# Down projection of a gated FFN: 512 output columns a PSUM bank in place of 256, and unit by unit over four banks in the second block of a pair

## The chip, the cores and the metric

The kernel runs on one core of a Trainium2 chip. The metric is the device time of one execution in microseconds. Three executions of the kernel before took 2626.48, 2628.86 and 2635.57 us (median 2628.86). The profile is of one further execution, which took 2622.47 us; the span between its first and last instruction is 2620.6 us.

The engines are named as in the profile: PE (TensorE, matmuls; PEld is its weight loads), DVE (VectorE), ACT (ScalarE), POOL (GpSimd) and SP (the queue that issues most loads).

## The reference

One decoder step over a prompt of 2048 rows (plus 16 meta rows) and 8 sample rows, model width 1024. After the mixer comes a gated convolutional FFN of width 2816, and its last product is the place of this change:

```python
def conv_ffn(x, w_up, conv_w, conv_b, w_down, buf):
    l = x.shape[1]
    hid = x @ w_up
    a, v = hid[..., :D_FF], hid[..., D_FF:]
    ext = jnp.concatenate([buf.astype(a.dtype), a], axis=1)
    c = conv_b + sum(ext[:, j:j + l] * conv_w[j] for j in range(CONV_W))
    y = (jax.nn.silu(c) * v) @ w_down
    return y, ext[:, -(CONV_W - 1):]

def block(h, ...):
    ...
    yf, conv = conv_ffn(rms_norm(h, norm_ffn_g), ffn_w_up, ffn_conv_w, ffn_conv_b, ffn_w_down, conv0)
    return h + yf, s5r, s5i, hg, conv
```

A final RMSNorm of `h + yf` gives `y_prompt` (2048 x 1024) and `y_sample` (8 x 1024). All of it is float32.

## The kernel before

The prompt is cut into four blocks of 512 rows. The FFN is computed for two blocks at a time (`ffn(p2)`, first pair: blocks 0 and 1, second pair: blocks 2 and 3). In the code that pair is `blks`, and `ex` is true in the first pair, which also carries the 8 sample rows.

Every float32 operand is split into a rounded part and its rest: `split_w` (L446) makes `wh` on ACT (L449) and `wl` on DVE (L83) from a staged weight tile `st`; activations are `ah` and `al`, the gated product is `gh` and `gl`. A product is then three matmuls (`PASS`, L470): wh with gh, wh with gl, wl with gh. A weight tile that is loaded, split and used is called a unit (`w_unit`, L456): at most 128 x 1024 elements. There are two buffers of `st`, three of `wh` and three of `wl`.

The 2816 FFN columns are 22 tiles of 128, taken in six parts (`FPARTS`, L32: four of four tiles, two of three). For each part the up projection (`up`, `fm_mm`, matmuls at L480, up to 512 columns each, one PSUM bank of the pool `mm` at a time) gives `gh` and `gl` of the part for both blocks. Then the down projection adds the part's share to `hacc` (L1197 to L1218). Before the change it runs over four quarters of 256 output columns. A unit holds the part's tiles times 256 columns. For each block, two row tiles of 128 share a bank of 512: `tm_mm` (matmuls at L500) fills its left half with 12 matmuls (9 in parts of three tiles), then its right half, and DVE adds the bank to `hacc` (L80). In the very last part of the second pair the quarters are grouped as (0), (1, 2, 3), so that `finish` (the final norm and the output) of the first row tiles can begin early. In the first pair the sample rows follow each quarter as 40 stationary columns (`ex_mm`, L514; 40 = 8 high parts, padding, 8 low parts).

Where the first pair ends, the norms of blocks 2 and 3 (`norm2`, transposes at L547 into the pool `tp`) are asked for before the last down projection, and their instructions stand between its matmuls.

PSUM has eight banks: three of `mm` (`bank`), two of `tp` (`tbank`), three of `hg` (`gbank`); the FFN of the kernel before uses none of `hg`. The order of the instructions on each engine is made by a scheduler from the program and its dependencies, not by the order of the code alone.

Of the kernel before, what the change touches and what calls it, by code (L numbers as in the profile page):

```python
# [27 lines left out]
NF = 22  # L28
# [9 lines left out]
def kernel(  # L38
# [28 lines left out]
    def ap(t, off, pat):  # L67
        return bass.AP(tensor=t.tensor, offset=t.offset + off, ap=pat)
# [7 lines left out]
    mm = nc.tensor.matmul  # L76
    f_ = lambda a: a.bitcast(F32)

    def add(o, a, b):
        tt_(o, a, b, op=OP.add)  # L80
# [7 lines left out]
    def bank():  # L88
        return ps.tile([128, 512], F32, name="mm")
# [17 lines left out]
    def scr(shape=None):  # L107
        return shaped(nt.tile([128, 512], F32, name="nt"), shape)

    def v3(t, a, b):  # L110
        return t[:, :a * b].rearrange("p (a b) -> p a b", a=a)
# [334 lines left out]
    def split_w(st, n):  # L446
        hi = wp.tile([128, 1024], F32R, name="wh", bufs=3)
        lo = wp.tile([128, 1024], F32R, name="wl", bufs=3)
        ACT(hi[:, :n], st[:, :n], AF.Copy)  # L449
        sub(lo[:, :n], st[:, :n], f_(hi[:, :n]))  # L450
        return hi, lo

    def w_stage():
        return wp.tile([128, 1024], F32, name="st", bufs=2)

    def w_unit(src, k0, nk, c0, ncol):  # L456
        st = w_stage()
        rs = src.shape[1]
        dma_w(v3(st, nk, ncol), ap(src, k0 * 128 * rs + c0, [[rs, 128], [128 * rs, nk], [1, ncol]]))
        hi, lo = split_w(st, nk * ncol)  # L460
        return v3(hi, nk, ncol), v3(lo, nk, ncol)

    win, wglu, wout, wup, wdn = w_in[0], s5_w_glu[0], w_out[0], ffn_w_up[0], ffn_w_down[0]
# [6 lines left out]
    PASS = ((0, 0), (0, 1), (1, 0))  # L470
# [15 lines left out]
    def behind(ins, prev):  # L486

        if prev is not None:
            tc.add_manual_dep(ins.ins, prev.ins.name, mybir.DependencyInfo(
                mybir.DependencyClass.NoSync, mybir.DependencyReason.DATA), reason="bank shared by groups")  # L490
        return ins

    def tm_mm(dst, wu, nks, lhs, prev):

        i, tot = 0, 3 * sum(nks)
        k = 0
        for (hi, lo), nk in zip(wu, nks):
            for kk in range(nk):
                for wi, ai in PASS:
                    o = mm(dst, lhs(ai, k), (hi, lo)[wi][:, kk, :], start=(i == 0), stop=(i == tot - 1))  # L500
                    if i == 0:
                        behind(o, prev)
                    i += 1
                k += 1
        return o

    def ex_mm(dst, wu, nks, stat, m):

        i, tot = 0, 2 * sum(nks)
        k = 0  # L510
        for (hi, lo), nk in zip(wu, nks):
            for kk in range(nk):
                for w in (hi, lo):
                    mm(dst[:m], stat[:, k, :m], w[:, kk, :], start=(i == 0), stop=(i == tot - 1))  # L514
                    i += 1
                k += 1
# [9 lines left out]
    def norm_rows(x, m, sq=None):  # L526
        ss = sm.tile([128, 1], F32, name="ss", bufs=6)
        if sq is None:
            sq = scr().bitcast(mybir.dt.bfloat16)[:, :D]
        ACT(sq[:m], x[:m] if len(sq.shape) == 2 else v3(x, 8, 128)[:m], AF.Square, accum_out=ss[:m])  # L530
        return rstd_of(ss[:m], 1, 1.0 / D)
# [49 lines left out]
    def ex_sum(p, m, off, n):  # L581

        t = scr()[:m, :n]
        ACT(t, p[off:off + m, :n], AF.Copy)
        return t
# [504 lines left out]
    def ffn(p2):  # L1090
        blks = (2 * p2, 2 * p2 + 1)
        ex = p2 == 0
        acts, hacc = [F2[b] for b in blks], []
        if ex:
            hE = ex2.tile([10, D], F32, name="hE")
# [14 lines left out]
        def finish(b, ha, t):  # L1110
            r = norm_rows(ha[:, t], 128)
            stt(ha[:, t], ha[:, t], r, fng, op0=OP.mult, op1=OP.mult)
            (dma if ex else dma_w)(y_prompt[0, b * BT + t * 128:b * BT + t * 128 + 128, :], ha[:, t])

        def conv_tail():
            po = tbank()
            nc.tensor.transpose(po[:44, :128], aC.rearrange("p f j -> p (f j)"), ident)
            so = scr()[:44, :128]
            nc.vector.tensor_copy(so, po[:44, :128])
            dma(cv_p[0, 0].rearrange("j (f p) -> f j p", p=128), so)  # L1120

        for f0, f1 in FPARTS:
            nf = f1 - f0
            gs = {}
# [43 lines left out]
            if f0 == 0:  # L1168
                for b in blks:
                    ha = hp.tile([128, 4, D], F32, name="hacc")  # L1170
# [5 lines left out]
            if ex:  # L1176
# [11 lines left out]
                gst = ex2.tile([128, 4, 40], F32R, name="gst")  # L1188
# [3 lines left out]
            if f1 == NF:  # L1192
                fng = x4()
                dma_w(fng, ap(final_norm_g, 0, [[0, 128], [1, D]]))
                if not ex:
                    conv_tail()
            for qg in ((0,), (1, 2, 3)) if f1 == NF and not ex else ((0,), (1,), (2,), (3,)):  # L1197
                wus = [(slice(256 * q, 256 * q + 256), [w_unit(wdn, f0, nf, 256 * q, 256)]) for q in qg]
                for b, ha in zip(blks, hacc):
                    for t2_ in range(2):  # L1200
                        for qs, wu in wus:
                            p = v3(bank(), 2, 256)
                            o = None
                            for i in range(2):
                                t = 2 * t2_ + i
                                o = tm_mm(p[:, i, :], wu, (nf,),
                                          lambda ai, k: gs[b, f0 + k][ai][:, t * 128:t * 128 + 128], o)
                            hs = ha[:, 2 * t2_:2 * t2_ + 2, qs]
                            add(hs, hs, p)
                        if qg[-1] == 3 and f1 == NF:  # L1210
                            finish(b, ha, 2 * t2_)
                            finish(b, ha, 2 * t2_ + 1)
                for qs, wu in wus if ex else ():
                    pe = bank()
                    ex_mm(pe[:, :256], wu, (nf,), gst, 40)
                    t = ex_sum(pe, 8, 32, 256)
                    add(t, pe[:8, :256], t)
                    add(hE[0:8, qs], hE[0:8, qs], t)  # L1218
        if ex:
            r = norm_rows(hE, 8)  # L1220
            stt(hE[0:8], hE[0:8], r, fng[0:8], op0=OP.mult, op1=OP.mult)
# [11 lines left out]
    for p2 in range(2):  # L1233
        ffn(p2)
# [34 lines left out]
```

## Time and profile before

| | |
|---|---|
| median of three executions | 2628.86 us (2626.48 to 2635.57) |
| the profiled execution | 2622.47 us, span 2620.6 us, 39925 instructions |
| PE busy | 2496.9 us, 95% of the span |
| PEld, DVE, ACT, POOL busy | 86%, 56%, 34%, 6% |
| chain that ended last, by engine | PE 72%, DVE 11%, ACT 4%, DMA 3%, issue 3% |
| chain, by line | L480 (up projection and other products) 41%, L500 (down projection and others) 25% |
| TensorE's clock over the span | 0.987 of full speed |

How to read it: the busy time of PE is that of a pipeline. A matmul starts before the one ahead of it has ended, so the durations of single matmuls overlap, and the pace of the engine is the distance from one start to the next. The chain lists runs of matmuls with the time they took together, from which that distance follows. The two lines of the chain are helpers; L500 serves the FFN's down projection and, earlier, the mixer's products, and the names of the operands tell them apart (gh and gl are the FFN's).

### The profile page before, as it was taken

The page shows a single profiled execution, that of the slowest core. Times are in us where ns is not written, and L with a number is a line of the kernel's source. Part 1 is how long each engine was busy: PE and PEld are TensorE (multiplying, and loading weights), DVE is VectorE, ACT ScalarE, POOL GpSimd, SP SyncE. Part 2 cuts the span into 40 slices and gives each one's busy share as a digit, 9 for nine tenths or more (in the row PEclk, how much of TensorE's full clock was granted, in tenths as well). Part 3 has the DMA queues.
Part 4 walks back from the last instruction along what each step waited for, and adds up shares of the span by engine and source line. Part 5 has one row for each costly group of instructions (what it writes and reads, how often), then busy time and mean ns, then how long its engine had stood idle before and what let it go on. Part 6 is the DMA issues. An engine that isn't in the chain of part 4 may idle for free.

```text
span 2620.6 us, 39925 instructions
## 1 busy us (share of the span) xinstructions
PE 2496.9 (95%) x16515; PEld 2263.8 (86%) x16515; DVE 1456.0 (56%) x2978; ACT 903.6 (34%) x1564; POOL 166.2 (6%) x254
## 2 busy tenths in 40 slices
PE   7887998999999999999999999999999999999998
PEld 6786876888888888989999999999889898989887
DVE  6875697678669688553333333345843333343344
ACT  3553344434425445341313131223531313131222
POOL 1232100100000001000000000000300000000000
PEclk9997999999999999999999999999999999999999
DMA  4345433553564662731111111111521111111111
GB/s 126 103 138 184 98 111 133 153 167 121 132 197 131 168 219 86 247 92 49 49 45 45 49 48 42 43 47 57 195 73 49 49 49 49 49 49 49 41 48 74
DMA packets 274939, 252.50 MB, mean 96 GB/s; under 512 B 11367, under 2 KB 255999, under 8 KB 270654
## 3 DMA queue, kind: packets, MB, share of 16 engines
q1 hardware_dynamic: 264680, 220.42, 27.9%
q0 software_dynamic: 9904, 29.48, 3.5%
q8 instruction: 129, 2.11, 0.3%
q14 instruction: 52, 0.43, 0.1%
q10 hardware_dynamic: 174, 0.06, 0.0%
HBM read 216.41 MB, written 33.27 MB: 95 GB/s over the span
## 4 chain that ended last, share of the span: by engine, by line
PE 72%; DVE 11%; ACT 4%; DMA 3%; issue 3%; POOL 1%; SPq 0%; POOLq 0%; ACTq 0%; DVEq 0%
PE mm L480 41%; PE mm L500 25%; DVE wl L83 1%; DVE hf L632 1%; PE mm L514 1%; DMA st<-in_w_out_dram 1%; POOL rstd L521 1%; DVE sB L86 1%; DMA st<-in_w_in_dram 1%; PE tp L899 1%; ACT wh L449 1%; DVE sA L885 1%; DVE al L83 1%; PE tp L847 1%; DVE sA L86 1%
## 5 line engine op out<-in xcount | busy, mean ns | idle before, releaser
L480 PE MATMUL mm<-ah,wh 128*128 128x512 f32 (+3 forms) x2320 | 817.6, 353 | 5.1 <-ACT ah L552 3.8
L480 PE MATMUL mm<-al,wh 128*128 128x512 f32 (+3 forms) x2320 | 814.6, 351 | 1.1 <-DVE al L83 1.1
L480 PE MATMUL mm<-ah,wl 128*128 128x512 f32 (+3 forms) x2320 | 814.9, 351 | 0.5 <-DVE wl L83 0.5
L449 ACT ACTIVATE wh<-st 128x1024 fp32r<-128x1024 f32 (+1 forms) x264 | 275.7, 1046 | 859.8 <-PE mm L480 315.5
L480 PEld LDWEIGHTS mm<-ah,wh 128*128 128x128 f32 x2320 | 441.1, 190 | 60.0 <-ACT ah L552 4.5
L480 PEld LDWEIGHTS mm<-ah,wl 128*128 128x128 f32 x2320 | 441.1, 190 | 55.7 <-DVE wl L83 1.0
L480 PEld LDWEIGHTS mm<-al,wh 128*128 128x128 f32 x2320 | 441.0, 190 | 54.6 <-DVE al L83 1.6
L83 DVE TENSOR_TENSOR wl<-st,wh 128x1024 fp32r<-128x1024 f32 (+1 forms) x264 | 318.1, 1206 | 272.6 <-ACT wh L449 271.4
L500 PE MATMUL mm<-wh,gh 128*128 128x256 f32 x1408 | 399.6, 284 | 2.0 <-DVE hacc L80 1.5
L500 PE MATMUL mm<-wh,gl 128*128 128x256 f32 x1408 | 399.5, 284 | 0.0
L500 PE MATMUL mm<-wl,gh 128*128 128x256 f32 x1408 | 399.2, 284 | 0.0
L500 PE MATMUL mm<-wh,ah 128*128 128x256 f32 x1024 | 291.7, 286 | 7.3 <-ACT hg L671 3.2
L500 PE MATMUL mm<-wh,al 128*128 128x256 f32 x1024 | 290.9, 284 | 5.8 <-DVE al L83 5.0
L500 PE MATMUL mm<-wl,ah 128*128 128x256 f32 x1024 | 289.0, 284 | 1.2 <-DVE wl L83 1.2
L80 DVE TENSOR_TENSOR hacc<-hacc,mm 128x512 f32<-128x512 f32 x192 | 131.3, 685 | 267.1 <-PE mm L500 267.0
L500 PEld LDWEIGHTS mm<-wh,gh 128*128 128x128 f32 x1408 | 270.9, 192 | 3.0 <-DVE hacc L80 1.7
L500 PEld LDWEIGHTS mm<-wh,gl 128*128 128x128 f32 x1408 | 270.8, 192 | 0.4
L500 PEld LDWEIGHTS mm<-wl,gh 128*128 128x128 f32 x1408 | 271.0, 192 | 0.0
L500 PEld LDWEIGHTS mm<-wh,ah 128*128 128x128 f32 x1024 | 194.7, 191 | 10.3 <-ACT hg L671 3.4
L500 PEld LDWEIGHTS mm<-wh,al 128*128 128x128 f32 x1024 | 195.2, 191 | 8.4 <-DVE al L83 6.2
L500 PEld LDWEIGHTS mm<-wl,ah 128*128 128x128 f32 x1024 | 194.8, 191 | 2.1 <-DVE wl L83 1.8
L86 DVE TENSOR_TENSOR c<-c,mm 128x512 f32<-128x512 f32 (+1 forms) x110 | 63.7, 579 | 215.6 <-PE mm L480 214.3
(377 smaller groups left out, 2606.0 us busy)
## 6 DMA issues: line engine op xcount, KB each, us to landing
st<-in_ffn_w_up_dram SPq DMA_DIRECT2D x96, 512.0 KB
big<-tab_d SPq DMA_DIRECT2D x32, 1156.0 KB
st<-in_w_in_dram SPq DMA_DIRECT2D x48, 512.0 KB
st<-in_w_in_dram SPq DMA_DIRECT2D x64, 256.0 KB
st<-in_w_out_dram SPq DMA_DIRECT2D x32, 512.0 KB
st<-in_ffn_w_down_dram SPq DMA_DIRECT2D x32, 512.0 KB
x<-in_x_prompt_dram SPq DMA_DIRECT2D x30, 512.0 KB
h_d<-x POOLq DMA_DIRECT2D x16, 512.0 KB, 4.8
```

The costliest lines, as they stand in the source:

```text
L80: tt_(o, a, b, op=OP.add)
L83: tt_(o, a, b, op=OP.subtract)
L86: tt_(o, a, b, op=OP.mult)
L449: ACT(hi[:, :n], st[:, :n], AF.Copy)
L480: mm(p[:, :n], w[wi][:, k, :], a[ai][:, k, c0:c0 + n], start=(i == 0), stop=(i == 3 * nk - 1))
L500: o = mm(dst, lhs(ai, k), (hi, lo)[wi][:, kk, :], start=(i == 0), stop=(i == tot - 1))
L514: mm(dst[:m], stat[:, k, :m], w[:, kk, :], start=(i == 0), stop=(i == tot - 1))
L521: nc.gpsimd.tensor_tensor(r, r, mhalf[:ss.shape[0], :n], op=OP.pow)
L632: nc.vector.reciprocal(R[:, c0:c1], P[:, c0:c1])
L847: mm(pes[i // ng][:, i % ng, :], Bk[:, i, :], UT[:, i // 2, :nj], start=True, stop=True)
L885: nc.vector.tensor_tensor_scan(out=G[:, i, 1:129], data0=sv[:, RHO, g:g + 1].to_broadcast([128, 128]), data1=xr[:, i, :], initial=Hc[:, g: ...
L899: o = mm(py[:, 2 * i:2 * i + 2, :].rearrange("p a b -> p (a b)"), G[:, 2 * i + j, 0:128], Cm[:, 2 * i + j, :], start=False, stop=(j == 1))
```

## The change

The down projection goes over two halves of 512 output columns in place of four quarters of 256. Each half has two units: up to two tiles of the part times 512 columns (in parts of three tiles, one unit of two tiles and one of a single tile). Each row tile of 128 has a bank of its own, taken by turns from the pools `mm` and `hg`, so four row tiles of a block hold four banks. In the first block of a pair (and in the second half of the very last part) a row tile goes over both units before the next row tile begins. In the second block the first unit goes over all four row tiles, and then the second. The sample rows follow the first block with 512 columns. `finish` is called for one row tile at a time, after its add in the second half of the last part. The new matmuls are at L1209.

```diff
--- before.py
+++ after.py
@@ -1194,28 +1194,44 @@
                 dma_w(fng, ap(final_norm_g, 0, [[0, 128], [1, D]]))
                 if not ex:
                     conv_tail()
-            for qg in ((0,), (1, 2, 3)) if f1 == NF and not ex else ((0,), (1,), (2,), (3,)):
-                wus = [(slice(256 * q, 256 * q + 256), [w_unit(wdn, f0, nf, 256 * q, 256)]) for q in qg]
+            end = f1 == NF and not ex
+            for q in range(2):
+                qs = slice(512 * q, 512 * q + 512)
+                ks = [k for k in range(0, nf, 2)]
+                wus = [w_unit(wdn, f0 + k, min(2, nf - k), 512 * q, 512) for k in ks]
                 for b, ha in zip(blks, hacc):
-                    for t2_ in range(2):
-                        for qs, wu in wus:
-                            p = v3(bank(), 2, 256)
-                            o = None
-                            for i in range(2):
-                                t = 2 * t2_ + i
-                                o = tm_mm(p[:, i, :], wu, (nf,),
-                                          lambda ai, k: gs[b, f0 + k][ai][:, t * 128:t * 128 + 128], o)
-                            hs = ha[:, 2 * t2_:2 * t2_ + 2, qs]
-                            add(hs, hs, p)
-                        if qg[-1] == 3 and f1 == NF:
-                            finish(b, ha, 2 * t2_)
-                            finish(b, ha, 2 * t2_ + 1)
-                for qs, wu in wus if ex else ():
-                    pe = bank()
-                    ex_mm(pe[:, :256], wu, (nf,), gst, 40)
-                    t = ex_sum(pe, 8, 32, 256)
-                    add(t, pe[:8, :256], t)
-                    add(hE[0:8, qs], hE[0:8, qs], t)
+                    ps_ = [(bank, gbank)[t % 2]() for t in range(4)]
+
+                    def part(i, t):
+                        for kk in range(min(2, nf - ks[i])):
+                            k = ks[i] + kk
+                            for j, (wi, ai) in enumerate(PASS):
+                                mm(ps_[t], gs[b, f0 + k][ai][:, t * 128:t * 128 + 128], wus[i][wi][:, kk, :],
+                                   start=(k == 0 and j == 0), stop=(k == nf - 1 and j == 2))
+
+                    def done(t):
+                        add(ha[:, t, qs], ha[:, t, qs], ps_[t])
+                        if f1 == NF and q == 1:
+                            finish(b, ha, t)
+
+                    if b == blks[0] or end and q == 1:
+                        for t in range(4):
+                            for i in range(len(ks)):
+                                part(i, t)
+                            done(t)
+                    else:
+
+                        for i in range(len(ks)):
+                            for t in range(4):
+                                part(i, t)
+                                if i == len(ks) - 1:
+                                    done(t)
+                    if ex and b == blks[0]:
+                        pe = bank()
+                        ex_mm(pe, wus, [min(2, nf - k) for k in ks], gst, 40)
+                        t = ex_sum(pe, 8, 32, 512)
+                        add(t, pe[:8], t)
+                        add(hE[0:8, qs], hE[0:8, qs], t)
         if ex:
             r = norm_rows(hE, 8)
             stt(hE[0:8], hE[0:8], r, fng[0:8], op0=OP.mult, op1=OP.mult)
```

On DVE, at the first down projection of the second pair: before, the adds of both blocks stand together (hacc_18926 and hacc_18928 are blocks 2 and 3), and a split of weights (wl) follows each quarter.

```order
L83 TENSOR_TENSOR wl_19153<-st_19150,wh_19152 128x1024
L83 TENSOR_TENSOR gl1_18923<-c_18852,gh1_18922 128x512
L80 TENSOR_TENSOR hacc_18926<-hacc_18926,mm_18936 128x2x256
L80 TENSOR_TENSOR hacc_18926<-hacc_18926,mm_18962 128x2x256
L80 TENSOR_TENSOR hacc_18928<-hacc_18928,mm_18988 128x2x256
L80 TENSOR_TENSOR hacc_18928<-hacc_18928,mm_19014 128x2x256
L83 TENSOR_TENSOR wl_19263<-st_19260,wh_19262 128x1024
L80 TENSOR_TENSOR hacc_18926<-hacc_18926,mm_19046 128x2x256
L80 TENSOR_TENSOR hacc_18926<-hacc_18926,mm_19072 128x2x256
L80 TENSOR_TENSOR hacc_18928<-hacc_18928,mm_19098 128x2x256
```

After, in the same place: hacc_17722 and hacc_17724 are blocks 2 and 3, wl_17859 is the second unit of the second half.

```order
L83 TENSOR_TENSOR wl_17853<-st_17850,wh_17852 128x1024
L83 TENSOR_TENSOR gl1_17719<-c_17648,gh1_17718 128x512
L80 TENSOR_TENSOR hacc_17722<-hacc_17722,mm_17738 128x512
L80 TENSOR_TENSOR hacc_17722<-hacc_17722,hg_17739 128x512
L80 TENSOR_TENSOR hacc_17722<-hacc_17722,mm_17740 128x512
L80 TENSOR_TENSOR hacc_17722<-hacc_17722,hg_17741 128x512
L83 TENSOR_TENSOR wl_17859<-st_17856,wh_17858 128x1024
L80 TENSOR_TENSOR hacc_17724<-hacc_17724,mm_17794 128x512
L80 TENSOR_TENSOR hacc_17724<-hacc_17724,hg_17795 128x512
L80 TENSOR_TENSOR hacc_17724<-hacc_17724,mm_17796 128x512
L80 TENSOR_TENSOR hacc_17724<-hacc_17724,hg_17797 128x512
L83 TENSOR_TENSOR wl_17977<-st_17974,wh_17976 128x1024
```

That split now stands between the adds of the two blocks, ahead of the second block's.

On PE, in the second block of that part: before, twelve matmuls go into the left half of one bank, with one unit (wh_18932, wl_18933) and the four tiles of gh1 and gl1.

```order
L500 MATMUL mm_18988<-wh_18932,gh1_18502 128x256
L500 MATMUL mm_18988<-wh_18932,gl1_18503 128x256
L500 MATMUL mm_18988<-wl_18933,gh1_18502 128x256
L500 MATMUL mm_18988<-wh_18932,gh1_18642 128x256
L500 MATMUL mm_18988<-wh_18932,gl1_18643 128x256
L500 MATMUL mm_18988<-wl_18933,gh1_18642 128x256
...
L500 MATMUL mm_18988<-wh_18932,gh1_18922 128x256
L500 MATMUL mm_18988<-wh_18932,gl1_18923 128x256
L500 MATMUL mm_18988<-wl_18933,gh1_18922 128x256
L500 MATMUL mm_18988<-wh_18932,gh1_18502 128x256
```

After, the first unit (wh_17728, wl_17729) gives six matmuls of 512 columns to bank mm_17794, then six to hg_17795, and the bank mm_17794 is entered again with the second unit (wh_17734, wl_17735).

```order
L1209 MATMUL mm_17794<-wh_17728,gh1_17298 128x512
L1209 MATMUL mm_17794<-wh_17728,gl1_17299 128x512
L1209 MATMUL mm_17794<-wl_17729,gh1_17298 128x512
...
L1209 MATMUL mm_17794<-wl_17729,gh1_17438 128x512
L1209 MATMUL hg_17795<-wh_17728,gh1_17298 128x512
L1209 MATMUL hg_17795<-wh_17728,gl1_17299 128x512
L1209 MATMUL hg_17795<-wl_17729,gh1_17298 128x512
...
L1209 MATMUL mm_17794<-wh_17734,gh1_17578 128x512
L1209 MATMUL mm_17794<-wh_17734,gl1_17579 128x512
L1209 MATMUL mm_17794<-wl_17735,gh1_17578 128x512
```

The bank changes after six matmuls, and each bank is left and entered once more before its add.

On DVE, at the end of the program: before, two row tiles are finished behind the last two adds.

```order
L80 TENSOR_TENSOR hacc_18928<-hacc_18928,mm_23913 128x2x256
L80 TENSOR_TENSOR hacc_18928<-hacc_18928,mm_23933 128x2x256
L520 TENSOR_SCALAR rstd_23956<-ss_23953 128x1
L1112 SCALAR_TENSOR_TENSOR hacc_18928<-hacc_18928,rstd_23956,x4_23554 128x1024
L520 TENSOR_SCALAR rstd_23964<-ss_23961 128x1
L1112 SCALAR_TENSOR_TENSOR hacc_18928<-hacc_18928,rstd_23964,x4_23554 128x1024
```

After, one row tile stands behind the last add.

```order
L520 TENSOR_SCALAR rstd_21686<-ss_21683 128x1
L80 TENSOR_TENSOR hacc_17724<-hacc_17724,hg_21636 128x512
L1112 SCALAR_TENSOR_TENSOR hacc_17724<-hacc_17724,rstd_21686,x4_21438 128x1024
L520 TENSOR_SCALAR rstd_21704<-ss_21701 128x1
L1112 SCALAR_TENSOR_TENSOR hacc_17724<-hacc_17724,rstd_21704,x4_21438 128x1024
```

The scaling of the row tile before it (rstd_21686) has moved behind that add.

## Rows read from the trace of the kernel before

**Rows 1.** Windows; columns: stretch, length, busy us (instructions) by engine, PEclk, DMA

```profile
1181.40:2607.80 1426.40, 1422.38 (x9172) 1303.21 (x9171) 596.84 (x1025) 381.62 (x556) 35.05 (x60) 1.00 0.18 56
0.00:1181.40 1181.40, 1074.55 (x7344) 960.55 (x7345) 855.16 (x1948) 519.76 (x1004) 130.05 (x192) 0.98 0.48 145
```

**Rows 2.** The chain that ended last, in order of time: start, us, what

```profile
1181.60 11.51 PE mm L500 x96
1194.04 11.51 PE mm L500 x96
...
1962.41 46.07 PE mm L500 x384
...
2141.62 87.07 PE mm L480 x384
```

**Rows 3.** Groups by line and form on PE: count, busy us, mean ns, idle before

```profile
L480 PE MATMUL mm<-ah,wh 128*128 128x512 f32 x1392 | 549.1, 394 | 0.3 <-ACT wh L449 0.2
...
L500 PE MATMUL mm<-wh,gh 128*128 128x256 f32 x1408 | 399.6, 284 | 2.0 <-DVE hacc L80 1.5 <-DVE nt L80 0.5
...
L514 PE MATMUL mm<-wh,gst 128*40 128x256 f32 x88 | 21.7, 279 | 0.0
```

**Rows 4.** Timeline of PE, L480 at 256 columns: start, us, instruction

```profile
1662.31 0.28 PE L480 MATMUL mm<-ah,wh 128*128 128x256 f32 x1
...
1664.91 0.28 PE L480 MATMUL mm<-al,wh 128*128 128x256 f32 x1
```

**Rows 5.** Timeline of PE, a group left for transposes and entered again

```profile
1825.20 0.66 PE L547 MATMUL tp<-ident,x 128*128 128x128 f32 x4
1825.62 0.36 PE L500 MATMUL mm<-wl,gh 128*128 128x256 f32 x1
1825.82 0.28 PE L500 MATMUL mm<-wh,gh 128*128 128x256 f32 x1
```

**Rows 6.** Timeline at a quarter of part 1 of the second pair

```profile
1973.84 1.06 ACT L449 ACTIVATE wh<-st 128x1024 fp32r<-128x1024 f32 x1 [10.04 <-PE mm L500]
...
1973.96 0.69 DVE L80 TENSOR_TENSOR hacc<-hacc,mm 128x512 f32<-128x512 f32 x1 [2.19 <-PE mm L500]
...
1974.93 1.23 DVE L83 TENSOR_TENSOR wl<-st,wh 128x1024 fp32r<-128x1024 f32 x1 [0.28 <-ACT wh L449]
```

**Rows 7.** Windows at the end of the first pair, columns as in rows 1

```profile
1823.80:1875.50 51.70, 47.76 (x381) 46.12 (x380) 43.19 (x77) 26.82 (x47) 7.21 (x11) 0.97 0.42 130
1846.00:1856.00 10.00, 7.42 (x58) 6.74 (x58) 9.27 (x17) 5.82 (x10) 1.10 (x2) 1.00 0.41 126
1856.00:1858.00 2.00, 1.32 (x8) 1.07 (x9) 2.00 (x5) 1.49 (x3) 0.00 (x0) 0.94 1.01 267
1858.00:1859.00 1.00, 1.00 (x7) 1.00 (x6) 1.00 (x4) 0.00 (x0) 0.00 (x0) 0.50 0.98 292
1861.00:1862.00 1.00, 1.00 (x10) 1.00 (x9) 0.52 (x1) 0.00 (x0) 0.00 (x0) 0.92 0.00 0
```

**Rows 8.** Timeline of the tail, behind the last matmul

```profile
2607.44 0.28 PE L500 MATMUL mm<-wl,gh 128*128 128x256 f32 x1
2607.78 1.27 DVE L80 TENSOR_TENSOR hacc<-hacc,mm 128x512 f32<-128x512 f32 x2
...
2609.15 1.06 ACT L530 ACTIVATE nt<-hacc 128x1024 bf16<-128x1024 f32 x1 [4.52 <-DVE hacc L80]
...
2610.33 0.15 DVE L520 TENSOR_SCALAR rstd<-ss 128x1 f32<-128x1 f32 x1 [1.27 <-ACT nt L530]
2610.63 0.55 POOL L521 TENSOR_TENSOR rstd<-rstd,mhalf 128x1 f32<-128x1 f32 x1 [4.09 <-DVE rstd L520]
...
2611.21 1.28 DVE L1112 SCALAR_TENSOR_TENSOR hacc<-hacc,rstd,x 128x1024 f32<-128x1024 f32 x1 [0.73 <-POOL rstd L521]
...
2613.29 1.28 DVE L1112 SCALAR_TENSOR_TENSOR hacc<-hacc,rstd,x 128x1024 f32<-128x1024 f32 x1 [0.73 <-POOL rstd L521]
```

**Rows 9.** The tile hacc: durations ns min/median/max, first and last start

```profile
L80 DVE TENSOR_TENSOR hacc<-hacc,mm x192: 666/687/690, 1184.5 to 2608.4; 128x512 f32<-128x512 f32 x192
```

## The prediction

> **What bounds the kernel now.** I read the engines' busy time by stretches first. From 1181.4 us (first down projection) to 2607.8 the multiplies of TensorE are busy 1422.4 of 1426.4 us at the full granted clock, while VectorE has 597 and ScalarE 382 [rows 1]: this half of the run is as long as the spacing of its matmuls. Nothing before 1181.4 us is touched. The chain of waits comes next; it shows the spacing itself. 384 matmuls of L500 (256 columns) take 46.07 us, 384 of L480 (512 columns) 87.07 us [rows 2]: 119.97 and 226.74 ns. So 256 more columns cost 106.8 ns (0.417 ns each, the 2.4 GHz level), and 13.2 ns of each matmul belong to the instruction and not to its columns. The duration of one (284 and 394 ns, [rows 3]) is a latency, since the next starts long before it ends. Last I read what waits at the two places where TensorE is not full: the end of the first pair (norms of blocks 2 and 3 stand in the last down projection) and the tail after the last matmul.
>
> **What goes.** 4224 matmuls of 256 columns (three groups of 1408, [rows 3]) become 2112 of 512. Two old ones take 239.94 ns, a new one 226.74: 13.2 ns saved, 2112 times, is 27.9 us. All of it lies on the path, as TensorE has no other idle time there. The new spacing is taken from L480, where weights stand still and activations move; in L500 and L1209 it is the other way round. That this makes no difference is shown by L480 at 256 columns: 22 spacings from 1662.31 to 1664.91, 118 ns each [rows 4], as in L500.
>
> The sample rows: 176 matmuls of 40x256 (two groups of 88, [rows 3]) become 88. Eight take 0.93 us now (from 1193.11, the end of 96 matmuls, to 1194.04, [rows 2]), 116 ns each; with 106.8 ns more for the columns a new one takes 223 against 232: 9 ns, 88 times, 0.8 us.
>
> **What is added.** Reopening of banks. In the second block of a pair each unit goes over four open banks, six matmuls (three in a unit of one tile) at a time, so each bank is left and entered again: four re-entries a half, in 23 halves (12 parts of two, less the very last), 92 in all. The trace has a few re-entries: an L500 group is left for four transposes at 1825.20, and the first matmul after them has 0.20 us to the next in place of 0.12 [rows 5]. Taken whole, that is 92 x 0.08 = 7.4 us; but the transposes change the kind of operand too, and a change of bank alone costs nothing: 96 matmuls over four banks keep 11.51 us, the same 119.9 ns [rows 2]. I take 0, and keep 7.4 for the range.
>
> Two units a half instead of one a quarter: the same 48 splits in number, and nearly the same elements. Three buffers of wh and wl now hold the two open units and one ahead. So the fourth unit of a part (the second of its second half) can only be split when the first unit is done, in the middle of the second block. From then it takes 1.06 us on ScalarE, and 1.23 on VectorE that ends 2.3 us after the start [rows 6]. It stands on VectorE ahead of the four adds of that block (the order above), so it waits for no add. TensorE wants it after the rest of the block and six matmuls of the next half: 24 + 6 spacings, 6.8 us, or 12 + 6, 4.1 us, in parts of three tiles. Slack of 4.4 and 1.7 us: cost 0. Were it queued behind the adds, it would come at 0.7 + 1.2 us after the block's end [rows 6, 9], against a third matmul of that unit at 1.8: about 0.1 to 0.6 us in each of 12 parts, 7 at most. What it does delay is the first add of the block, by about 1 us, and the bank of that add is next opened some 20 matmuls into the following half: cost 0. The adds are 192 of 512 columns before and after, at 0.687 us [rows 9]; six banks in place of three only loosen their wait. SP's loads are still four a part; a st buffer comes free with its split, so the load behind the fourth unit's split is issued in the middle of that second block, a whole half (over 20 us) before the next split needs it: cost 0.
>
> **The end of the first pair.** From 1823.8 to 1875.5 VectorE is busy 43.2 of 51.7 us and TensorE idle for 3.9; in 1846 to 1856 VectorE has 9.3 of 10 and TensorE 7.4 [rows 7]. In such a stretch fewer matmul cycles bring nothing by themselves. This part's share of the sum is 144 x 13.2 ns = 1.9 us; I take 1.0 back. Bounds: the 3.9 us of idle time vanish with six banks, or as much again is added, since the transposes now stand at other places between the matmuls.
>
> **The tail.** Now the last matmul starts at 2607.44 and ends 0.28 later; then two adds, square, reciprocal root and scaling of two row tiles, and the output [rows 8]: 12.9 us to the end of the span. In the changed order each row tile is finished by itself, so behind the last matmul stands one tile: one add (0.6) and one round of the chain (2611.21 to 2613.29, 2.1) less: 2.7 us. Against it: a tile comes every 9 x 0.2267 = 2.04 us, and VectorE's round is up to 0.88 (2610.33 to 2611.21) + 1.28 = 2.16, so over seven tiles it may fall behind by 0.8. I take 2.2, of 1.9 to 2.7.
>
> **Sum.** -27.9 - 0.8 + 1.0 - 2.2 = -29.9 us against the profiled execution's 2622.47 (span 2620.6): 2592.6. That execution lies 6.4 us under the median of 2628.86, which the same sum takes to 2599.0, my forecast: 1.1% faster. Some 0.3% (7.9 us) is what a measurement of this kernel can tell from no change.
>
> **Rivals.** *The fixed share is not fixed*: the time that L500 spends beyond its columns grows with the columns, and a matmul of 512 takes 2 x 119.97. For: no 512-column matmul with moving weights is in the trace. Against: [rows 4] and the exact 0.417 ns a column. Only the tail is left: 2626.7.
>
> The Trainium skill ("TensorE: Matmul & The Clock Gate", Back-to-back issue gap) gives, for a single warm gap, the columns over 2.4 GHz plus 2.5 ns, so 109.2 and 215.8 ns; by it the gain is an estimated 2112 x 2.5 ns = 5.3 us, and with the tail the time is 2621.4. The trace's 119.97 and 226.74 do not agree, and decide.
>
> *The clock falls in the second blocks* (the slower side). If the hops between four banks leave TensorE small gaps, its clock may fall as it does at 1858, after the stretch with 7.4 of 10 us busy: 0.94, 0.50 and 0.92 granted in the stretches from there to 1862 (three of one microsecond at 0.50), which is 0.12 + 1.5 + 0.08 = 1.7 us lost [rows 7]. One fall in each of the 23 halves is 39 us, more than the gain: 2599 + 39 = 2638. It decides from 18 falls on. Against it: every operand and bank is ready early by the slacks above, and between 1181.4 and 2607.8 the clock's mean is 1.00 [rows 1].
>
> The Trainium skill ("TensorE: Matmul & The Clock Gate", A second HAM failure mode: psum-queue depth-cycling) tells of just this: 512-column matmuls that cycle through banks idle a little between groups and the clock swings. No stretch of this trace shows it without a wait of VectorE's beside it.
>
> *The costs kept at nothing are paid*: re-entries 7.4 and the end of the first pair 4 us. Then 2599 + 11 = 2610, still faster.
>
> **Chances.** Forecast 0.80; costs paid 0.09 (faster too); not fixed, or 2.5 ns of it, 0.06 (within 0.3%); clock falls 0.05 (slower). So faster 0.89, same 0.06, slower 0.05. The range reaches from 2588 (the fastest execution shown with the whole sum, 2592.6, less the 3.9 us of idle time and 0.5 of the tail) to 2612 (costs paid, and 2 us of spread).
>
> **What would show it.** The 384 matmuls of a part become 192 of L1209, in 43.5 us in place of 46.07; if it stays at 46, the first rival is right. TensorE busy without gaps at the change of half, wl of the fourth unit ending over 4 us before its first use. Granted clock 1.00 in the second blocks. From the last matmul to the end about 10.7 us. From 1181.4 to the last matmul about 1399 us in place of 1426. A VectorE or ScalarE wait of TensorE at L1209 of over 0.5 us in many parts would make the prediction wrong.

## The result and the profile after

The changed kernel takes 2593.59 us (median of 4 runs, 2588.76 to 2598.71) beside 2627.67 us for the kernel before: a ratio of 0.9869, 95% interval 0.9851 to 0.9887. The prediction was 2599.0 us (a ratio of 0.9886) with a range of 2588 to 2612. The profiled execution took 2598.71 us, its span 2597.0.

Windows of the changed kernel (columns as in [rows 1]): the part before the first down projection, then from there to the last matmul, then the end of the first pair, and the three short stretches that answer to [rows 7].

```profile
0.00:1194.10 1194.10, 1083.55 (x7344) 968.46 (x7345) 855.46 (x1948) 520.00 (x1005) 130.49 (x192) 0.96 0.48 143
1194.10:2586.50 1392.40, 1392.18 (x6972) 1181.01 (x6970) 594.28 (x1001) 382.29 (x546) 36.36 (x60) 1.00 0.18 57
1824.67:1868.32 43.65, 43.43 (x223) 35.04 (x222) 41.03 (x71) 25.82 (x44) 8.56 (x11) 1.00 0.45 145
1846.00:1856.00 10.00, 10.00 (x54) 8.37 (x53) 9.95 (x19) 6.86 (x12) 1.10 (x2) 1.00 0.30 108
1856.00:1858.00 2.00, 2.00 (x11) 1.42 (x10) 2.00 (x5) 0.70 (x2) 0.00 (x0) 1.00 0.73 256
1858.00:1859.00 1.00, 1.00 (x6) 0.68 (x5) 1.00 (x3) 0.00 (x0) 0.00 (x0) 1.00 0.03 12
```

TensorE was idle for 4.0 us between the first down matmul and the last one [rows 1], and now is idle for 0.22. The stretch is 1392.1 us from the start of the first matmul (1194.1) to the start of the last (2586.19), where it was 1426.0 (1181.4 to 2607.44, [rows 1, 8]). From the start of the last matmul to the end of the span it is 10.8 us in place of 13.2. Together the two are 36.3 us less. The span is only 23.6 us shorter, because the first down matmul starts 12.7 us later, in a part that the diff doesn't touch; its mean granted clock was 0.96 in this execution and 0.98 in the one before.

The chain that ended last, in order of time (start, us, what). It shows the first block, the sample rows, the end of the first pair, and one half of the second pair with its second block.

```profile
1194.27 2.72 PE mm L1209 x12
1196.99 2.72 PE hg L1209 x12
...
1205.15 1.85 PE mm L514 x8
...
1757.02 67.65 PE mm L480 x432
...
1868.32 87.09 PE mm L480 x384
1955.41 2.72 PE mm L1209 x12
...
1966.29 1.36 PE mm L1209 x6
1967.65 1.36 PE hg L1209 x6
...
1975.81 1.36 PE hg L1209 x6
1977.17 2.72 PE mm L1209 x12
```

Twelve matmuls of 512 columns take 2.72 us, 226.7 ns each, in the first block; in the second block the 48 from 1966.29 to 1977.17, with a change of bank behind every sixth, take 10.88 us, the same 226.7 ns. Eight sample matmuls of 512 columns take 1.85 us, 231 ns each. The end of the first pair reaches from the end of 432 matmuls (1757.02 + 67.65 = 1824.67) to 1868.32.

VectorE at the change of half in the second pair (start, us, instruction, then idle time before it and what ended that), which answers to [rows 6]:

```profile
1972.63 1.23 DVE L83 TENSOR_TENSOR wl<-st,wh 128x1024 fp32r<-128x1024 f32 x1 [5.62 <-ACT wh L449]
1973.77 0.68 DVE L80 TENSOR_TENSOR hacc<-hacc,mm 128x512 f32<-128x512 f32 x1
1974.49 0.69 DVE L80 TENSOR_TENSOR hacc<-hacc,hg 128x512 f32<-128x512 f32 x1
```

The split of the fourth unit ends at 1973.86, ahead of the four adds. TensorE needs it six matmuls into the next half, at 1978.5: 4.7 us early. From the first down matmul to the last TensorE waits once, 0.2 us for a normed tile at L547.

The tail (same columns):

```profile
2586.19 0.39 PE L1209 MATMUL hg<-wl,gh 128*128 128x512 f32 x1
...
2586.79 0.68 DVE L80 TENSOR_TENSOR hacc<-hacc,hg 128x512 f32<-128x512 f32 x1
...
2587.57 1.06 ACT L530 ACTIVATE nt<-hacc 128x1024 bf16<-128x1024 f32 x1 [0.92 <-DVE hacc L80]
2587.61 1.28 DVE L1112 SCALAR_TENSOR_TENSOR hacc<-hacc,rstd,x 128x1024 f32<-128x1024 f32 x1
...
2589.10 0.55 POOL L521 TENSOR_TENSOR rstd<-rstd,mhalf 128x1 f32<-128x1 f32 x1 [1.52 <-DVE rstd L520]
2589.68 1.28 DVE L1112 SCALAR_TENSOR_TENSOR hacc<-hacc,rstd,x 128x1024 f32<-128x1024 f32 x1 [0.73 <-POOL rstd L521]
```

One add and one whole round of the chain stand behind the last matmul, where [rows 8] had two of each; of the row tile before it only the end of its round is left, with the scaling at 2587.61.

### The profile page after: what moved, and what is told of

It reads as the page before. It is cut to its first block, busy times and chain, and to the rows that moved or that the text cites. A ratio compares the mean times of both kernels' runs of the same rounds, so it can differ in the third digit from the quotient of the medians.

```text
span 2597.0 us, 35488 instructions
## 1 busy us (share of the span) xinstructions
PE 2475.8 (95%) x14315; PEld 2149.5 (83%) x14315; DVE 1453.3 (56%) x2954; ACT 903.6 (35%) x1552; POOL 167.9 (6%) x254
## 4 chain that ended last, share of the span: by engine, by line
PE 72%; DVE 10%; issue 4%; ACT 3%; DMA 3%; POOL 1%; SPq 0%; POOLq 0%; ACTq 0%; DVEq 0%
PE mm L480 42%; PE mm L1209 9%; PE hg L1209 9%; PE mm L500 7%; DVE hf L632 1%; PE mm L514 1%; DVE wl L83 1%; DVE sB L86 1%; POOL rstd L521 1%; DVE sA L885 1%; PE tp L899 1%; DMA st<-in_w_in_dram 1%; DVE sA L86 1%; PE tp L547 1%; PE tp L847 1%
## 5 line engine op out<-in xcount | busy, mean ns | idle before, releaser
L480 PE MATMUL mm<-ah,wh 128*128 128x512 f32 (+3 forms) x2320 | 819.8, 353 | 4.5 <-ACT ah L552 3.3
L480 PE MATMUL mm<-al,wh 128*128 128x512 f32 (+3 forms) x2320 | 816.6, 352 | 1.1 <-DVE al L83 1.1
L480 PE MATMUL mm<-ah,wl 128*128 128x512 f32 (+3 forms) x2320 | 816.5, 352 | 0.5 <-DVE wl L83 0.5
L480 PEld LDWEIGHTS mm<-ah,wh 128*128 128x128 f32 x2320 | 442.5, 191 | 60.3 <-ACT ah L552 3.9
L480 PEld LDWEIGHTS mm<-ah,wl 128*128 128x128 f32 x2320 | 442.1, 191 | 55.9 <-DVE wl L83 1.0
L480 PEld LDWEIGHTS mm<-al,wh 128*128 128x128 f32 x2320 | 442.2, 191 | 55.2 <-DVE al L83 1.6
L1209 PE MATMUL mm<-wh,gh 128*128 128x512 f32 x352 | 137.5, 391 | 0.0
L1209 PE MATMUL hg<-wh,gl 128*128 128x512 f32 x352 | 137.2, 390 | 0.0
L1209 PE MATMUL hg<-wl,gh 128*128 128x512 f32 x352 | 137.2, 390 | 0.0
L1209 PE MATMUL mm<-wh,gl 128*128 128x512 f32 x352 | 137.2, 390 | 0.0
L1209 PE MATMUL mm<-wl,gh 128*128 128x512 f32 x352 | 137.2, 390 | 0.0
L1209 PE MATMUL hg<-wh,gh 128*128 128x512 f32 x352 | 137.1, 389 | 0.0
L80 DVE TENSOR_TENSOR hacc<-hacc,hg 128x512 f32<-128x512 f32 x96 | 65.8, 686 | 88.2 <-PE hg L1209 87.7
```

The costliest lines, as they stand in the source:

```text
L480: mm(p[:, :n], w[wi][:, k, :], a[ai][:, k, c0:c0 + n], start=(i == 0), stop=(i == 3 * nk - 1))
L1209: mm(ps_[t], gs[b, f0 + k][ai][:, t * 128:t * 128 + 128], wus[i][wi][:, kk, :], start=(k == 0 and j == 0), stop=(k == nf - 1 and j == 2))
```

## Experiments

The theory at this point: the gain is the 13.2 ns that each matmul costs beside its columns, and the part that the prediction missed (the end of the first pair) comes from six banks in place of three. The rivals: the order over four banks does it, or the clock.

**The changed kernel again, and the second block row tile by row tile.**

> The changed kernel once more, as the yardstick for the others of this chip. It was 1.3% faster than before. The stretch from the first matmul of the down projection to the last should again be about 1392 us (1426 before), the end of the first pair about 43.7 us (51.5 before) with no clock fall, the tail 10.6 us; if one of the three is far from that, it was chance in the profiled execution.

> As the changed kernel, but the second block too goes row tile by row tile (both units, then the next row tile), so no bank is left and entered again. Theory: the order of units over open banks costs and brings nothing. The fourth unit of a part is freed 6 matmuls (1.36 us) before the second block's end, its split takes 2.3 us, and it is wanted 1.8 us after that end, so TensorE does not wait: within 0.3% of the changed kernel, 48 matmuls of the second block still 10.88 us. Rival: the order hides the split; without it TensorE waits 0.5 to 1 us at each of 12 changes of half: 6 to 12 us slower than the changed kernel.

```diff
-                    if b == blks[0] or end and q == 1:
+                    if True:
```

The unedited kernel took 2587.05 us (5 runs, ratio 0.9843, 0.9824 to 0.9862), the edited one 2593.3 us (4 runs, ratio 0.9862, 0.9842 to 0.9882); the intervals overlap. The traces agree closer than the times: 1392.2 and 1392.8 us from the first to the last down matmul, 43.8 and 44.4 us at the end of the first pair. The waits of TensorE in the down projection of the edited kernel (engine and line, waited for: us, times, longest) are one:

```profile
PE mm L1209 <- ACT wh L449: 0.8, 1, 0.8
```

So the order over four open banks costs nothing and brings at most this one wait of 0.8 us, where 6 to 12 us would have spoken for the rival. In both kernels the first down matmul starts at 1182.3, where the kernel before has 1181.4: the 12.7 us of the first profile don't come with the change.

**Six banks in the kernel before.**

> The kernel before with 256 columns as it was; only the banks of its down projection are taken by turns from two pools (six banks in place of three). Theory: the banks are what freed the end of the first pair (3.9 us idle and 1.7 us of clock fall gone there), so that stretch goes from 51.5 to 46 us and nothing else moves: 2622, 5 us faster than before. Rival 1: the fall of the end of the first pair came from the shorter matmul work and its new order, then the stretch stays at 51 and the time at 2627. Rival 2: the banks bring the whole gain: 2594.

```diff
-                            p = v3(bank(), 2, 256)
+                            p = v3((bank, gbank)[t2_](), 2, 256)
```

2622.32 us (11 runs), ratio 0.9976 (0.9966 to 0.9986). The end of the first pair in its windows, and all waits of TensorE from the first down matmul to the last:

```profile
1829.69:1875.77 46.08, 45.35 (x379) 44.60 (x378) 43.77 (x78) 27.51 (x49) 7.97 (x11) 1.00 0.48 149
```

```profile
PE mm L500 <- DVE hacc L80: 0.7, 1, 0.7
```

The same waits in the kernel before:

```profile
PE mm L500 <- DVE hacc L80: 1.5, 1, 1.5
PE tp L1226 <- DVE nt L86: 1.1, 1, 1.1
PE tp L547 <- DVE rstd L520: 0.8, 2, 0.5
PE mm L500 <- DVE nt L80: 0.5, 1, 0.5
```

With matmuls of 256 columns still, the stretch falls from 51.5 us (chain of the kernel before, 1823.8 to 1875.3) to 46.1; TensorE's idle time falls from 3.9 us to 0.7 and the stretch of lowered clock is gone. So six banks are worth 5.4 us there, of the 7.9 that the change gains. The run does not part the banks from the order of instructions that the scheduler makes with them: the two transposes of L1226, for which TensorE waited 1.1 us before, now stand behind the last matmul of the part, as they do in the changed kernel, and the last transposes of L547 stand 24 matmuls later.

**The changed kernel with each matmul in two halves of 256.** The order is that of the row-tile kernel, and the banks stay six.

> As the kernel with row tile order in both blocks, but every matmul of 512 columns is two of 256 (left half of the bank, then right half): units, banks, loads and adds stay as changed, only the number of matmuls goes back to 4224. Theory (13.2 ns of each matmul do not depend on its columns): 27.9 us slower than the changed kernel, about 2621, 240 ns for two. Rival (banks, units and order bring the gain): no slower than the changed kernel.

```diff
+                            for h in range(2):
+                                hs = slice(256 * h, 256 * h + 256)
...
+                                        x = mm(ps_[t][:, hs], gs[b, f0 + k][ai][:, t * 128:t * 128 + 128],
+                                               wus[i][wi][:, kk, hs], start=(k == 0 and j == 0),
```

2624.53 us (12 runs), ratio 0.9981 (0.9968 to 0.9993). Its chain:

```profile
1199.55 2.88 PE mm L1225 x24
1202.43 2.88 PE hg L1225 x24
```

24 matmuls of 256 take 2.88 us, 120 ns each, and the stretch from the first to the last is 1422.5 us, 29.7 more than the row-tile kernel's 1392.8. Of these, 2.2 stand at the end of the first pair (46.6 against 44.4) and 27.5 elsewhere (the count of matmuls makes 26.0 there; the other 1.5 are not accounted for); the doubled number of matmuls takes the gain of the width back. What is left of the change is small: the ratio of 0.9981 is 3.4 us against the kernel before of that run (2627.96).

**Quarters of 128: is the share fixed?** The edit is made on the kernel with halves, so the order is again that of the row-tile kernel.

> The changed kernel with each 512-column matmul of the down projection issued as four of 128 columns (8448 instead of 2112 matmuls, the same columns in all). Theory, a fixed share on top of the columns: 256 columns took 119.97 ns and 512 took 226.74 ns, so 128 should take 53.4 + 13.2 = 66.6 ns; four take 266.4 instead of 226.7 ns, 2112 x 39.7 ns = +83.8 us, so 2671 to 2678 us against the 2587 to 2594 us of the changed kernel. Rival, the weight load sets the pace once the matmul is too short to cover it: 128 columns take as long as 256 did, 120 ns at most, and the time goes up by as much as 2112 x (480 - 226.7) = 535 us, to about 3125 us; anything clearly above 2700 us speaks for a floor of this sort. By the Trainium skill, TensorE: Matmul & The Clock Gate, Back-to-back issue gap, a matmul of 128 columns in such a stream would be an estimated 81 ns, which would give +205 us.

```diff
-                            for h in range(2):
-                                hs = slice(256 * h, 256 * h + 256)
+                            for h in range(4):
+                                hs = slice(128 * h, 128 * h + 128)
```

The two runs took 3191.64 and 3253.28 us, beside 2628.97 for the kernel before. The theory's fixed share falls: the time is far above 2700. The rival's floor (120 ns at most) is found, but its 3125 us is too low, because a fall of TensorE's clock came on top that neither had. The chain, the windows (columns as in [rows 1]) and a wait of TensorE in the execution of 3191.64 us:

```profile
1612.50 10.24 PE mm L1225 x48
1622.74 10.24 PE hg L1225 x48
1635.78 5.31 PE mm L1225 x48
1641.09 5.36 PE hg L1225 x48
```

```profile
1186.45:1207.80 21.35, 21.35 (x193) 21.34 (x193) 4.58 (x6) 1.46 (x2) 0.00 (x0) 1.00 0.09 25
2289.00:2359.00 70.00, 70.00 (x330) 70.00 (x330) 4.13 (x6) 0.64 (x1) 0.00 (x0) 0.50 0.00 0
```

```profile
PE mm L1225 <- DVE wl L83: 5.9, 8, 0.7
```

At the full clock 48 take 5.36 us, 111.7 ns each and not 66.6; where TensorE was granted 0.50, 1.2 GHz, 213 ns. The sum comes out within a few us: 8448 x 111.7 ns is 943.6 us against 2112 x 226.74 = 478.9, so +465; the clock is at 0.50 for 256 of the 1993 us from the first down matmul to the last (1186.3 to 3179.4), half of which, 128 us, is an estimate of what that cost; and TensorE is idle for 14 us there. Together 607; the stretch is 601 us longer than the changed kernel's. So the 13.2 ns hold between 256 and 512 columns and are not a law below that. That a matmul of 128 columns waits for its weight load is likely but not shown: in the first window the loads fill the time (21.34 of 21.35 us), but the matmuls do too.

The clock fell in the middle of a down projection four times, each time within 3 us behind one of the eight waits of 0.7 us for a split of weights (about 1593, 1793, 2281 and 2492); behind the other four it did not fall. It then stayed at 0.50 while TensorE was busy without a gap, and rose again only in or just behind matmuls of 512 columns, of the sample rows or of the next up projection. Whether the order of the changed kernel, in which no such wait occurs with 512 columns, would have kept the clock up was not tried.

By the Trainium skill (TensorE: Matmul & The Clock Gate, Back-to-back issue gap) a stream of loads and matmuls of 128 columns goes at about 81 ns; this run's 111.7 ns differs, and decides.

**The operands in bf16: whose are the 13.2 ns?**

> The changed kernel with the operands of the down projection (both pieces of the weights and of g) in bf16 instead of fp32r, so that they carry fewer bits; the number, width and order of the matmuls stay. It asks whose the fixed 13.2 ns are. Theory A, they belong to each pair of weight load and matmul whatever the type: 512 columns stay at 226.7 ns and the time at 2585 to 2594 us. Theory B, they belong to fp32r: the matmuls come nearer to their columns' own 213.5 ns, 2112 x 13.2 = up to 28 us less, 2559 to 2570 us. By the Trainium skill, TensorE: Matmul & The Clock Gate, Back-to-back issue gap, it would be an estimated 215.8 ns.

```diff
-                    hi = gp.tile([128, BT], F32R, name=f"gh{b % 2}")
-                    lo = gp.tile([128, BT], F32R, name=f"gl{b % 2}")
+                    hi = gp.tile([128, BT], B16, name=f"gh{b % 2}")
+                    lo = gp.tile([128, BT], B16, name=f"gl{b % 2}")
...
-                wus = [w_unit(wdn, f0 + k, min(2, nf - k), 512 * q, 512) for k in ks]
+                wus = [w_unit16(wdn, f0 + k, min(2, nf - k), 512 * q, 512) for k in ks]
```

`w_unit16` is `w_unit` with its two pieces in bf16; the sample rows' operand is bf16 as well. 2570.60 us (4 runs), ratio 0.9777 (0.9764 to 0.9791). Weight loads on TensorE's load row, first of the changed kernel, then of this one (count, duration ns min/median/max, first and last start), and this kernel's chain around one part:

```profile
L1209 PEld LDWEIGHTS mm<-wh,gh x352: 186/188/193, 1193.9 to 2583.5; 128*128 128x128 f32 x176
```

```profile
L1221 PEld LDWEIGHTS <-gh x1408: 95/98/99, 1182.1 to 2553.6; 128*128 128x128 bf16 x176
```

```profile
1975.73 87.06 PE mm L492 x384
2104.25 87.06 PE mm L492 x384
```

Between the end of one up projection (2062.79) and the start of the next (2104.25) stand 192 down matmuls: 215.9 ns each in place of 226.7. From the first to the last it is 1371.7 us, 20.5 less than the changed kernel's 1392.2. (2112 x 10.8 ns would be 22.8; the end of the first pair stayed at 43.6 us, with 0.9 us of waits.) So 10.8 of the 13.2 ns belong to fp32r, and theory A falls; the time of 2570.60 is just above the range of theory B. The weight load takes 188 ns in fp32r and 98 in bf16, but the run changed the type of both operands and does not show that the load is what costs the 10.8 ns. The 215.9 ns agree with the formula that the Trainium skill (TensorE: Matmul & The Clock Gate, Back-to-back issue gap) gives for a single gap, which makes 215.8; in fp32r the formula did not hold, and the about 131 ns that the section gives for 512 columns in a stream are reached in no run here.

**The last half unit by unit too.**

> The changed kernel with the last half of all run unit by unit too, so that its four banks end together and not one row tile after another. Theory: the work after the last matmul is a chain for each row tile (an add of 0.68 us, two ACT instructions of 1.25 us, the rstd on DVE and POOL, the scaling of 1.28 us, the write), and with the four rows ending within one last unit the last row's chain waits behind those of the others: the stretch from the last matmul to the end grows from 10.6 to 14 or 15 us. Rival: the DMA that ends the chain hides this, and the stretch stays within 1 us of 10.6.

```diff
-                    if b == blks[0] or end and q == 1:
+                    if b == blks[0]:
```

2599.42 us (one run). Its tail:

```profile
2583.82 0.39 PE L1209 MATMUL hg<-wl,gh 128*128 128x512 f32 x1
...
2585.06 1.29 DVE L1112 SCALAR_TENSOR_TENSOR hacc<-hacc,rstd,x 128x1024 f32<-128x1024 f32 x1
...
2587.14 2.48 DVE L1112 SCALAR_TENSOR_TENSOR hacc<-hacc,rstd,x 128x1024 f32<-128x1024 f32 x2 [0.67 <-POOL rstd L521]
...
2590.41 1.28 DVE L1112 SCALAR_TENSOR_TENSOR hacc<-hacc,rstd,x 128x1024 f32<-128x1024 f32 x1 [0.73 <-POOL rstd L521]
```

The stretch from the start of the last matmul to the end of the span (2597.7) is 13.9 us in place of 10.8 (2574.54 to 2585.3 in the repeated run): all four row tiles are scaled behind the last matmul, where the changed kernel scales two. The exception for the last half is worth 3.1 us; 13.9 is just under the 14 to 15 that were expected.

**The same tiling in the out projection of the mixer, alone and with bf16.** Two halves of 512 columns over four open banks (768 matmuls in place of 1536), first beside the kernel before, then on one chip with the changed kernel.

> The changed kernel with the same tiling carried to the out projection of the mixer: two halves of 512 columns, four units of two k-tiles each over four open banks, instead of four quarters of 256 columns (768 matmuls of 512 instead of 1536 of 256). Theory: each matmul saved is worth 13.2 ns, 768 x 13.2 = 10.1 us, so 2577 to 2584 us, a ratio of about 0.980 to the kernel before. Rival: this stage shares its banks and its input tiles with transposes and with DVE work, and four banks open at once take them away from those; the waits that this brings cost as much as the width saves or more, so 2587 to 2600 us, and new waits stand on the lines of the out projection or of the transposes behind it.

> The changed kernel once more, beside the two candidates on one chip. So far it took 2593.6 and 2587.1 us, ratios 0.9869 and 0.9843 to the kernel before; expected 2585 to 2594 us. How much of the gap between those two is the clock of the first 1180 us can be read from its windows.

> The kernel with the out projection in 512 columns once more, now beside the changed kernel on the same chip. Theory (768 matmuls saved, 13.2 ns each, less 2 to 5 us of new waits for ACT's split of its weights): 5 to 8 us below the changed kernel. Rival (the lower time of its first run was the chip's, not the kernel's): within 2 us of it.

> Out projection in 512 columns and down projection with operands in bf16 (which carry fewer bits) together. If the two gains lie in different stages they add: the down projection's 1392.2 us from first to last matmul become 1371.7, as with bf16 alone, and the first down matmul comes 5 to 8 us earlier, so 25 to 28 us below the changed kernel, 2560 to 2567 us. Rival: the shorter down projection runs into its weights' splits or the transposes behind it, and less than 20 us is left.

```diff
-        for q in range(4):
+        for q in range(2):
...
+            ps_ = [(bank, gbank)[t % 2]() for t in range(4)]
...
+            for kq in range(4):
+                hi, lo = w_unit(wout, 2 * kq, 2, 512 * q, 512)
+                for t in range(4):
```

First 2581.92 us (ratio 0.9824, 0.9811 to 0.9838). On one chip then: the changed kernel 2592.64 us (ratio 0.9869, 0.9852 to 0.9887), with the out projection 2582.20 (0.9828, 0.9812 to 0.9843), with both 2550.54 (0.9714, 0.9699 to 0.9728). Their first group of down matmuls (count, duration, first and last start), in this order:

```profile
L1209 PE MATMUL mm<-wh,gh x352: 387/389/481, 1189.9 to 2579.6; 128*128 128x512 f32 x176
```

```profile
L1224 PE MATMUL mm<-wh,gh x352: 387/390/481, 1179.0 to 2568.7; 128*128 128x512 f32 x176
```

```profile
L1236 PE MATMUL mm<-wh,gh x341: 377/379/391, 1161.9 to 2530.8; 128*128 128x512 bf16 x171
```

With the out projection alone the down projection starts 10.9 us earlier and lasts the same, and the times differ by 10.4 us: close to the 10.1 of 768 x 13.2 ns, and more than the 5 to 8 expected. That it is faster is clear in both measurements, but by how much is not: the start of the down projection varies by 13 us between executions of the same code (below). And new waits came, as the rival of the first run said (one line of the waits from 950 to 1175), so something beside the width may have paid for them; what it was is not known:

```profile
PE mm L999 <- ACT wh L449: 5.2, 2, 2.7
```

With both, the down projection's stretch is 1371.5 us, as expected. But its start comes 17 us earlier than with the out projection alone (13 earlier than the 1174.7 of that kernel's first run), and the time falls by 42 us in place of 25 to 28. The wait on ScalarE at L999 is not in that trace, and from 1050 to 1075 the granted clock is 1.00 where it was 0.86. Why the order of the mixer's end came out better there was not tried; part of it may be the spread of the first part (below). This last kernel beats the two that were compared, at the price of the bits that bf16 operands lose.

## Why the prediction was right, and where it missed

The stretch and the tail gave 36.3 us in the traces; the sum was 29.9.

- **Width, -27.9.** Right. The spacing is 226.7 ns. Outside the end of the first pair the stretch is 26.0 us shorter (33.9 - 7.9); the sum had 27.9 - 1.9 = 26.0 there. The halved matmuls give it back, 27.5 us. "From 1181.4 to the last matmul about 1399 us" measured 1392.
- **Sample rows, -0.8.** Nothing came of it: 231 ns is twice 116. The fixed share of the 128-column stationary operand isn't there with 40 columns, and the upper bound named in the prediction (232) was the true one.
- **Re-entry of banks, 0.** Right: 48 matmuls in 10.88 us, and the row-tile order has the same stretch within 0.6 us. The upper bound of 7.4 us from the transposes wasn't a cost of banks.
- **The fourth unit, 0.** Right: split 4.7 us ahead of its use; the 4.4 worked out.
- **The end of the first pair, +1.0 against a share of -1.9.** This is the step that failed, by size: 7.9 us were gained (51.5 to 43.65). The argument was that VectorE sets the time there, busy 9.3 of 10 us. It still is, 9.95 of 10 in the same window, but TensorE no longer waits for it. The run with six banks in the old kernel shows what was missed: with three banks, and the order that goes with them, TensorE could not go ahead far enough over the bursts of VectorE's work, and with six it can. The prediction had this as the far bound ("the 3.9 us of idle time vanish with six banks"), and left out that the fall of the clock that it priced at 1.7 us under a rival would go with the idle time. 3.9 + 1.7 + 1.9 = 7.5 of the 7.9. So VectorE's time was taken for a bound of this stretch, and 0.9 us of gain was forecast where 7.9 were measured. With operands in bf16 the stretch stayed at 43.6 us; whether VectorE bounds it from there on was not tried.
- **Tail, -2.2.** Right: 13.2 to 10.8, 2.4 less.
- **The rivals.** A share that grows with the columns fell with the spacing. The clock stayed at 1.00 from the first down matmul to the last. The costs kept at nothing were not paid.

The forecast of 2599.0 lies 5.4 us above the median, about the 6.4 us by which the sum was short. That the two come so close is partly luck: in the repeated runs the changed kernel stood at 2587.1 and 2592.6, and against the kernel before, the three measurements gave 34.1, 40.9 and 32.7 us. Most of the spread between executions lies in the part before the first down matmul, in which nothing was changed: the first down matmul started at 1181.4, 1187.3, 1194.1, 1182.3, 1189.9, 1182.3, 1193.6, 1191.8, 1186.3 and 1182.1 in ten traces whose first part is the same code (the kernel before and its version with six banks, the changed kernel in three runs, and five edits of its down projection), at mean granted clocks of 0.96 to 0.98.

## What to carry to other kernels

Where TensorE is full, read the spacing of matmuls at two widths in the same trace before anything else; the difference to the columns' own time, times the number of matmuls saved, is what wider tiles are worth. Here it held within 0.1 us in 26.0 when the matmuls were made wider and within 1.5 when they were halved again; carried on to 128 columns it failed. Ahead of a stretch where another engine seems to set the time, count the banks that let TensorE run ahead: VectorE's 9 in 10 with idle time on TensorE beside it was here, for the most part, a lack of banks and not a bound. And when an idle stretch with a lowered clock behind it goes, count both.

## What was not expected of the hardware

- In fp32r there is a floor: with 128 columns per matmul the spacing is 111.7 ns at 2.4 GHz, hardly under the 120 ns of 256 columns. With bf16 operands 512 columns take 215.9 ns in place of 226.7. Both fit a weight load that sets the pace; no run parts it from the rest.
- With 40 stationary columns the spacing of 256 and 512 columns is 116 and 231 ns, in proportion and without a fixed share, and the 512 take 4 ns longer than with 128 stationary columns. No run tells why.
- In the kernel with quarters a wait of 0.7 us stood ahead of each fall to 1.2 GHz in the middle of a down projection, and TensorE then stayed there though busy without a gap (the 70 us from 2289 above). Otherwise the clock stayed at 1.00 in the down projections, but for the end of the first pair: in the kernel before, the fall at 1858 [rows 7], and in the kernel with quarters, two more among the waits for the tiles that are transposed (L547, 7.2 us in all).
